# A hybrid attention and DeltaNet layer on one core: products of ones ahead of the tokens, norm weights spread by TensorE, the first head's K and V as plain products, and small products issued in groups

## The chip, the core and the metric

The kernel runs on one core of one Trainium2 chip. The metric is the device time of one execution in microseconds (us). The program lays out the inputs on the host beforehand; what is timed is one launch. In what follows PE is TensorE, DVE is VectorE, ACT is ScalarE, POOL is GpSimd and SP is SyncE, whose queue issues nearly all DMAs.

## The reference, cut to what matters

The layer takes 512 tokens of width 1024 and puts 16 learned meta tokens ahead of them, so L = 528. Everything is float32.

```python
hn = rms_norm(h, norm_w)                      # h: (1, 528, 1024)
proj = hn @ w_in                              # 1024 x 10256
aq, ak, av, az, dq, dk, dv, dz, db, da, ga, gd = split(proj)
...
s = q_blk . k * dh**-0.5                      # 8 heads, two maps of 64 each
p = softmax(where(causal, s, -inf))
o_a = (p[0] - lam * p[1]) @ v                 # differential attention
y_a = (rms_norm(o_a) * (1 - lam_init) * silu(az)) @ w_branch_attn
...
qkv = silu(causal_conv(concat(dq, dk, dv)))   # 4 taps, then l2-normalised q, k
v_new = u_c - w_c @ state                     # gated delta rule, chunk after chunk
o_c = qd_c @ state + a_c @ v_new
state = state * cd_c + kd_c.T @ v_new
y_d = (rms_norm(o_d) * silu(dz)) @ w_branch_delta
merged = sigmoid(ga) * y_a + sigmoid(gd) * y_d
out = rms_norm(h + merged @ w_out, final_norm_w)[:, 16:]
```

## The kernel before, in words

**Precision.** A float32 product is made of three fast passes. Each operand is split into a rounded high part and the rest: the tokens into `hnH` and `hnL`, each 512 KB block of weights (`raw`, 1024 inputs by 128 outputs) into `wh` (a copy by ACT) and `wl` (a subtraction by DVE). `PASSES` are high times high, high times low and low times high. A plain product of one block (`product`, and `first_products` for the first two blocks) walks over 8 slices of the inputs, three passes each, over the segments `FULL` of 272 and 256 tokens: 24 matmuls of 272 columns and 24 of 256.

**Pairs.** Two blocks whose number stands in `PAIRS` (line 60) go together through `pair_of_blocks`: seven half products in place of eight, in the manner of Strassen, of 264 columns each, from sums of tokens (`sumH`, `sumL`, made once by `token_sums`) and sums of weights, which DVE makes for each pair (`split_pair`). A pair takes 7 x 4 x 3 = 84 matmuls of 264 columns. The K and V blocks of the attention (`ak`, `av`) of every head are such a pair.

**Start.** `loads` (line 498) issues from SP's queue the first 128 tokens (`xt`), the norm weights spread over all partitions (`nwb`, 512 KB written to SBUF), the meta tokens (`mt`), the second 128 tokens, and then weights and tokens in turns. `normalise(n)` (line 526) takes the tokens as they land: ACT squares and sums a row, DVE scales the sum (`ss`), POOL takes the power (`rs`), DVE writes `dg`, the identity times `rs`; the inner task `weigh` multiplies `xt` by `nwb` on DVE; PE multiplies `xt` slice by slice with `dg`, which transposes and normalises in one; ACT copies the result to `hnH` and DVE subtracts to get `hnL`. n = 0 is the meta tokens, 1 to 4 are the 128-token pieces. `first_products` (line 1812) then starts the first two blocks (`dk` of heads 0 and 1) slice by slice as tokens come.

**Order of the work.** Every instruction is recorded through one helper, `Engine.emit`, so all rows of the profile have one line, L231 in this kernel. The program is written as tasks (Python generators) that say which engine, buffer or event they want next. A planner (`class Plan`) gives each instruction an estimated duration, takes over and over the task whose next step could begin earliest (`run`; equal times go by rank), and so writes the order in which instructions stand in each engine's queue. On the chip each engine runs its queue in that order and waits where an operand is late. `COLD` (line 80) is the planned time before which the planner counts PE's work double. Dense work (the products of tokens and weights) is one task of low priority, `dense`; attention (`attention`) and the delta rule (`delta_pair`, four pairs of heads) put small products of 128 columns or fewer, mostly between three dense passes, wherever their operands are planned to be there.

**Small chains.** In `delta_pair` a chunk's step runs from `S,kT` on PE over `vin` on DVE to `vin,TM` on PE, over `u` on ACT to `u,ktd` on PE, which gives the next state. In `attention`, `scores` writes `ak,aq` into the two-bank PSUM tile `psc`, ACT exponentiates to `e`, `combine` transposes and multiplies by `vs`, and the part of the meta tokens is `vm` times `pmT`.

**PSUM.** Six single banks go round under three kinds (`pd`, `pat`, `pdl`); `psc` is apart. `first_products` uses two banks for block 0 and `psc` for both segments of block 1.

## Time and profile before

| | |
|---|---|
| median of 3 runs | 757.45 us (757.4 to 757.57) |
| the profiled execution | 757.24 us |
| its span, first to last instruction | 755.5 us |
| PE busy | 735.5 us, 97% |
| DVE busy | 626.2 us, 83% |
| ACT busy | 498.6 us, 66% |
| first PE instruction | at 7.45 us |
| last PE instruction | begins at 748.89 us |

The span leaves 1.74 us of the profiled execution's time outside it. In the rows of the trace a first number is the start in us from the span's start, then the duration, engine, line, operation, output and inputs by the program's names, the tile (for a matmul the stationary part), and the output's shape; `xN` says that N records of one kind stand together, and a bracket tells how long the engine stood idle before and for what. A float32 matmul (`dg,xt`, `S,kT`) leaves two records, one per pass; a pass of the split products leaves one. Matmuls overlap, so what a pass costs is the distance from one start to the next, not its duration.

### The profile page before, as it was taken

The numbers are of one execution on the slowest core, as the hardware profiler recorded it, in microseconds if no ns is written. First come the engines' busy times: TensorE is split into PE (matmuls) and PEld (weight loads), VectorE is DVE, ScalarE is ACT, GpSimd is POOL, SyncE is SP. The second block draws the span as 40 slices with busy tenths as digits, with TensorE's granted clock in tenths as the row PEclk, the third lists the DMA queues.
The fourth block names the chain that finished last, engine by engine and source line by source line (L and its number), as shares of the span: only waits on it lengthen the run. The fifth ranks groups of instructions, "written<-read, shape, count | busy, mean of one in ns | idle before, by whom it ended". The sixth has DMA issues, their size and how long they took to land.

```text
span 755.5 us, 14370 instructions
## 1 busy us (share of the span) xinstructions
PE 735.5 (97%) x5311; PEld 668.6 (88%) x5311; DVE 626.2 (83%) x1431; ACT 498.6 (66%) x1322; POOL 74.7 (10%) x86
## 2 busy tenths in 40 slices
PE   5999999999999999999999999999999999999996
PEld 5998888899899899989989989988988998899875
DVE  6999999998889789879989888997479869797453
ACT  6369565879965678976767797767675445545132
POOL 3205000202000301100030210010000000000001
PEclk9999999999999999999999999999999999999998
DMA  8141321225314112521331152152141443132602
GB/s 306 57 133 33 114 80 64 64 71 158 97 42 140 34 53 85 169 78 52 110 79 59 36 180 85 56 202 65 49 147 57 141 130 121 56 118 90 239 4 109
DMA packets 45431, 74.88 MB, mean 99 GB/s; under 512 B 20728, under 2 KB 25636, under 8 KB 45360
## 3 DMA queue, kind: packets, MB, share of 16 engines
q1 hardware_dynamic: 45360, 73.95, 30.8%
q8 instruction: 42, 0.69, 0.4%
q14 instruction: 29, 0.24, 0.1%
HBM read 67.58 MB, written 6.36 MB: 98 GB/s over the span
## 4 chain that ended last, share of the span: by engine, by line
PE 83%; ACT 8%; DVE 4%; issue 2%; DMA 1%; POOL 0%; SPq 0%; POOLq 0%; ACTq 0%
PE bank L231 80%; PE psc L231 3%; ACT wh L231 2%; DVE wl L231 1%; ACT TM L231 1%; ACT ak L231 1%; DMA xt<-in_x_dram 1%; ACT vr L231 0%; DMA raw<-in_wblk_dram 0%; ACT bank L231 0%; ACT MT L231 0%; ACT e L231 0%; ACT aq L231 0%; ACT sqk L231 0%; DVE hnL L231 0%
## 5 line engine op out<-in xcount | busy, mean ns | idle before, releaser
L231 PE MATMUL bank<-hnH,wh 128*128 128x512 f32 (+4 forms) x664 | 233.4, 355 | 0.7 <-ACT hnH L231 0.7
L231 PE MATMUL bank<-hnH,wl 128*128 128x512 f32 (+4 forms) x664 | 221.6, 337 | 0.0
L231 PE MATMUL bank<-hnL,wh 128*128 128x512 f32 (+4 forms) x664 | 221.5, 337 | 0.0
L231 DVE TENSOR_TENSOR wl<-raw,wh 128x1024 fp32r<-128x1024 f32 (+1 forms) x120 | 134.9, 1126 | 24.6 <-ACT wh L231 24.1
L231 ACT CAST wh<-raw 128x1024 fp32r<-128x1024 f32 (+1 forms) x120 | 116.3, 971 | 43.4 <-PE bank L231 36.0
L231 PEld LDWEIGHTS bank<-hnH,wl 128*128 128x128 f32 x664 | 124.1, 188 | 13.9
L231 PEld LDWEIGHTS bank<-hnH,wh 128*128 128x128 f32 x664 | 124.5, 189 | 13.4 <-ACT hnH L231 0.9
L231 PEld LDWEIGHTS bank<-hnL,wh 128*128 128x128 f32 x664 | 124.4, 189 | 10.0
L231 PE MATMUL bank<-sumH,wh 128*128 128x264 f32 x224 | 68.5, 306 | 0.0
L231 PE MATMUL bank<-sumH,wl 128*128 128x264 f32 x224 | 63.6, 284 | 0.0
L231 PE MATMUL bank<-sumL,wh 128*128 128x264 f32 x224 | 63.5, 284 | 0.0
L231 DVE SCALAR_TENSOR_TENSOR y<-xp,pc,y 128x528 f32<-128x528 f32 (+1 forms) x72 | 54.0, 753 | 1.1 <-ACT y L231 1.0
L231 ACT ACTIVATE e<-psc,ast 128x144 f32<-128x144 f32 (+3 forms) x64 | 34.7, 543 | 21.5 <-DVE ast L231 18.3
L231 PEld LDWEIGHTS bank<-sumH,wh 128*128 128x128 f32 x224 | 42.3, 189 | 1.1 <-issue 0.6
L231 PEld LDWEIGHTS bank<-sumL,wh 128*128 128x128 f32 x224 | 42.4, 189 | 0.0
L231 PEld LDWEIGHTS bank<-sumH,wl 128*128 128x128 f32 x224 | 42.1, 188 | 0.0
L231 PE MATMUL bank<-btH,wh 128*128 128x256 f32 x128 | 36.1, 282 | 0.5 <-ACT sn L231 0.5
L231 PE MATMUL bank<-btH,wl 128*128 128x256 f32 x128 | 35.8, 280 | 0.0
L231 PE MATMUL bank<-btL,wh 128*128 128x256 f32 x128 | 35.8, 280 | 0.0
L231 ACT CAST wh<-st 128x1024 fp32r<-128x1024 f32 x22 | 23.1, 1048 | 13.0 <-PE bank L231 12.8
L231 PE MATMUL psc<-ak,aq 128*128 128x264 f32 (+3 forms) x160 | 29.7, 305 | 0.8 <-DVE aq L231 0.4
L231 DVE TENSOR_TENSOR wl<-st,wh 128x1024 fp32r<-128x1024 f32 x22 | 26.8, 1218 | 3.4 <-ACT wh L231 1.9
(373 smaller groups left out, 1699.5 us busy)
## 6 DMA issues: line engine op xcount, KB each, us to landing
raw<-in_wblk_dram SPq DMA_DIRECT2D x96, 512.0 KB, 3.5
raw<-in_wout_dram SPq DMA_DIRECT2D x8, 512.0 KB, 5.1
xt<-in_x_dram SPq DMA_DIRECT2D x4, 512.0 KB, 4.8
TM<-gcd SPq DMA_DIRECT2D x8, 256.0 KB, 5.2
xr<-in_x_dram SPq DMA_DIRECT2D x8, 256.0 KB, 6.3
out_dram<-xr SPq DMA_DIRECT2D x8, 256.0 KB, 2.5
room<-scrm SPq DMA_DIRECT2D x12, 128.0 KB, 3.3
oad<-room SPq DMA_DIRECT2D x6, 256.0 KB
```

What stands on the lines that cost most here:

```text
L231: return real(*args, **kw)
```

## The change

It has five parts.

1. The spread load of the norm weights is gone. One row of 4 KB (`nrow`) is loaded from ACT's queue as the kernel's first DMA. A new task, `norm_weights`, has PE multiply ones by ones eight times into `psc`, then spread the row over 128 partitions with two matmuls of a column of ones (K = 1) into the two banks of `psc`. `weigh` reads `psc`: the first 128 tokens in two halves, the others in one. `psc` is given back when all four are weighed.
2. `COLD` is 5200 in place of 10500, and the planner tells dense tasks from the others. While dense work can go on, small products wait until the dense run has lasted 300 ns (rank 0) or 900 ns (other ranks); after a small product, dense work is put off by 80 ns in the comparison; a change from small to dense is charged 85 ns.
3. The pair of `ak` and `av` of head 0 is out of `PAIRS`: the two blocks are plain products, and `after_a` copies them out.
4. `first_products` takes a single bank for block 1's first segment and waits for halves of `hnH`. `ss`, `rs` and `dg` have five buffers in place of three.
5. `combine` multiplies `vm` by `pmT` last and not first; `delta_pair` waits for the token sums' `t3` before it fetches `msub`.

```diff
-PAIRS = [n for n, (name, i) in enumerate(ORDER) if name == "ak" or name in ("dk", "dv") and i > 1 and i % 2 == 0]
+PAIRS = [n for n, (name, i) in enumerate(ORDER) if name == "ak" and i > 0 or name in ("dk", "dv") and i > 1 and i % 2 == 0]
...
-COLD = 10500
+COLD = 5200
+DENSE = ("dense", "rest_of_gates", "attention")
+SWITCH, RUNS, STAY = 85, (300, 900), 80
...
     def resume(self, task, engine, begin):
+        if engine == PE and self.dense(task) != self.run_kind:
+            self.run_kind, self.run_since = not self.run_kind, begin
+            begin += SWITCH * self.run_kind
...
+            steady = self.run_kind and any(
+                t.want == PE and self.dense(t) and t.time + (t.src != PE) * (self.HOP[t.src] + 80) <= self.free[PE]
+                for t in self.tasks)
...
-                key = max(t, self.free[eng]), task.rank
+                if eng == PE and steady and not self.dense(task):
+                    t = max(t, self.run_since + RUNS[task.rank > 0])
+                begin = max(t, self.free[eng])
+                key = begin + STAY * (eng == PE and not self.run_kind and self.dense(task)), task.rank
...
-    nwb = mk(sp, [P, D], F32, "nwb")
+    nrow = mk(sp, [1, D], F32, "nrow")
+    nc.scalar.dma_start(out=nrow, in_=prow[:, 1296:2320])
+    plan.events["nrow"] = 3200.0, SP
...
-                S.dma_start(out=nwb, in_=prow[:, 1296:2320].broadcast_to([P, D]))
-                done("nwb")
-                yield SP
...
-            yield "nwb"
-            yield DVE
-            V.tensor_tensor(out=xt[n], in0=xt[n], in1=mt[:, P:2 * P] if n == 0 else nwb, op=ALU.mult)
+            for c, w in ((0, 1), (1, 1)) if n == 1 else ((0, 2),):
+                for hf in range(c, c + w):
+                    yield f"norm weights {hf}"
+                yield DVE
+                t = xt[n][:, 512 * c:512 * (c + w)]
+                V.tensor_tensor(out=t, in0=t, in1=late["nw"][:, c:c + w].rearrange("p a t -> p (a t)"), op=ALU.mult)
             done(f"xw{n}")
+            if tick("weighed", NC):
+                give("psc")
...
+    def norm_weights():
+        yield ("psc",)
+        yield PE
+        nw = late["nw"] = bank("psc")
+        for _ in range(8):
+            T.matmul(nw[:, 0, 0:P], ones, ones, start=True, stop=True)
+        yield "nrow"
+        for hf in range(2):
+            yield PE
+            T.matmul(nw[:, hf], ones[0:1], nrow[:, 512 * hf:512 * hf + 512], start=True, stop=True)
+            done(f"norm weights {hf}")
...
+        yield "t3"
         msub = room[1].rearrange("p a t -> p (a t)")[:, 0:D].rearrange("p (j i) -> p j i", i=32)
...
-            T.matmul(po[:, 0:P], pmT, late["vm"], start=True, stop=False)
             for n in range(i + 1):
-                T.matmul(po[:, 0:P], pT[:, n, :], vs[:, n, :], start=False, stop=n == i)
+                T.matmul(po[:, 0:P], pT[:, n, :], vs[:, n, :], start=n == 0, stop=False)
+            T.matmul(po[:, 0:P], pmT, late["vm"], start=False, stop=True)
...
+    AFTER = dict(dk=after_dk, dv=after_dv, dq=after_dq, aq=after_aq, ak=lambda h, banks: after_a(h, banks, whole_ak),
+                 av=lambda h, banks: after_a(h, banks, whole_av))
```

The order that the planner writes changes over the whole length of PE's queue; the lines of the changed kernel read L252. Three places matter below. The first is the head of PE's queue. Before it reads as follows (`ss,samb` sums the meta tokens' squares, `dg,xt` transposes tokens, `wh` and `wl` belong to the first two blocks):

```order
L231 MATMUL bank_3_80<-ss_182,samb_96 128x1
...
L231 MATMUL bank_3_80<-dg_188,xt_123 128x128 x4
L231 MATMUL bank_4_81<-dg_188,xt_123 128x128 x4
L231 MATMUL bank_1_78<-hnH,wh_19_116 128x272 x8
L231 MATMUL bank_1_78<-hnH,wl_20_117 128x272 x3
L231 MATMUL bank_5_82<-dg_193,xt_124 128x128 x4
L231 MATMUL bank_6_83<-dg_193,xt_124 128x128 x4
L231 MATMUL bank_1_78<-hnH,wl_20_117 128x272 x5
L231 MATMUL bank_1_78<-hnL,wh_19_116 128x272 x8
L231 MATMUL psc_175<-hnH,wh_21_118 128x272 x3
L231 MATMUL bank_3_80<-dg_198,xt_125 128x128 x4
```

The same place in the changed kernel:

```order
L252 MATMUL psc_176<-ones 128x128 x8
L252 MATMUL psc_176<-nrow_84,ones 128x512 x2
...
L252 MATMUL bank_3_80<-dg_196,xt_124 128x128 x4
L252 MATMUL bank_4_81<-dg_196,xt_124 128x128 x4
L252 MATMUL bank_1_78<-hnH,wh_19_117 128x272 x7
L252 MATMUL bank_5_82<-dg_201,xt_125 128x128 x4
L252 MATMUL bank_6_83<-dg_201,xt_125 128x128 x4
L252 MATMUL bank_1_78<-hnH,wh_19_117 128x272
L252 MATMUL bank_1_78<-hnH,wl_20_118 128x272 x8
L252 MATMUL bank_1_78<-hnL,wh_19_117 128x272 x8
L252 MATMUL bank_3_80<-hnH,wh_21_119 128x272 x8
L252 MATMUL bank_3_80<-hnH,wl_22_120 128x272 x7
L252 MATMUL bank_4_81<-dg_206,xt_126 128x128 x4
```

Ten products stand ahead of everything, and between the second and the last piece of tokens 39 products of 272 columns stand where 27 stood.

The second place is the head of DVE's queue, from the weighing of the first tokens to the last `dg`. Before, the third piece's `dg_193` stands behind a `wl` and four `hnL`:

```order
L231 TENSOR_TENSOR hnL<-bank_4_81,hnH 128x4x128
L231 TENSOR_SCALAR ss_191<-ss_191 128x1
L231 TENSOR_TENSOR xt_124<-xt_124,nwb_84 128x1024
L231 TENSOR_TENSOR hnL<-bank_5_82,hnH 128x4x128
L231 TENSOR_TENSOR hnL<-bank_6_83,hnH 128x8x16
L231 TENSOR_TENSOR hnL<-bank_3_80,hnH 128x4x128
L231 TENSOR_TENSOR wl_22_119<-raw_15_112,wh_21_118 128x1024
L231 TENSOR_TENSOR hnL<-bank_4_81,hnH 128x4x128
L231 TENSOR_SCALAR dg_193<-ident,rs_192 128x128
```

In the changed kernel:

```order
L252 TENSOR_TENSOR hnL<-bank_4_81,hnH 128x4x128
L252 TENSOR_SCALAR ss_199<-ss_199 128x1
L252 TENSOR_TENSOR hnL<-bank_5_82,hnH 128x4x128
L252 TENSOR_TENSOR hnL<-bank_6_83,hnH 128x8x16
L252 TENSOR_SCALAR dg_201<-ident,rs_200 128x128
L252 TENSOR_TENSOR xt_125<-xt_125,psc_176 128x1024
L252 TENSOR_TENSOR hnL<-bank_3_80,hnH 128x4x128
L252 TENSOR_TENSOR hnL<-bank_4_81,hnH 128x4x128
L252 TENSOR_TENSOR wl_22_120<-raw_15_113,wh_21_119 128x1024
```

The third piece's `dg_201` has moved ahead of two `hnL`, the second `wl` and its own weighing; what stands up to the fourth piece's `dg` is the same work in both.

The third place is the first step of the delta rule on PE (`S` is the state, `kT` the keys, one of each head). Before, with dense passes (`hnH,wh` and the like) between:

```order
L231 MATMUL bank_6_83<-S_1769,kT_549 128x128
L231 MATMUL bank_1_78<-hnH,wh_19_116 128x264
L231 MATMUL bank_1_78<-hnL,wh_19_116 128x264
L231 MATMUL bank_1_78<-hnH,wl_20_117 128x264
L231 MATMUL bank_5_82<-S_1775,kT_604 128x128
L231 MATMUL bank_1_78<-hnH,wh_19_116 128x264
L231 MATMUL bank_1_78<-hnL,wh_19_116 128x264
L231 MATMUL bank_1_78<-hnH,wl_20_117 128x264
...
L231 MATMUL bank_6_83<-vin_1912,TM_680 128x128
L231 MATMUL bank_5_82<-vin_1915,TM_680 128x128
```

In the changed kernel:

```order
L252 MATMUL bank_6_83<-S_1750,kT_556 128x128
L252 MATMUL bank_5_82<-sumH_36_136,wh_23_121 128x264
L252 MATMUL bank_5_82<-sumL_40_140,wh_23_121 128x264
L252 MATMUL bank_5_82<-sumH_36_136,wl_24_122 128x264
L252 MATMUL bank_3_80<-S_1760,kT_597 128x128
L252 MATMUL bank_6_83<-vin_1881,TM_738 128x128
...
L252 MATMUL bank_3_80<-vin_1892,TM_738 128x128
```

The first head's `vin` stands directly behind the second head's `S,kT`, with three dense passes between it and its own `S,kT` where there were nine. Over the whole queue, runs of small products that stand between dense passes number 188 where there were 217.

More of the change, by code (lines that the diff above doesn't have):

```diff
@@ L142, in transfer, with dense @@
         self.arrival = self.dma + 900
+    def dense(self, task):
+        return task.gen.__name__ in DENSE and not task.other
     def resume(self, task, engine, begin):
+        if engine == PE and self.dense(task) != self.run_kind:
+            self.run_kind, self.run_since = not self.run_kind, begin
+            begin += SWITCH * self.run_kind
         self.task, self.engine, self.end, self.arrival = task, engine, begin, 0.0
@@ L982, in whole_av, with after_a @@
         done(f"av{h}")
+    def after_a(h, banks, then):
+        yield "ap"
+        yield ("vT",)
+        which = plan.task.slot
+        for j in range(2):
+            yield banks.event(j)
+            yield ACT
+            pd, t0, w = banks[j]
+            A.copy(out=late["vT"][which][:, t0:t0 + w], in_=pd)
+            give("pd", pd)
+        yield from then(h, which)
     kt_, s_, sd_, vs_, qe_ = 0, 1, 2, 3, 4
@@ L1812, in first_products @@
     def first_products():
-        yield ("psc",)
-        sc = bank("psc")
-        dst = [[], (sc[:, 0, :], sc[:, 1, :])]
+        dst = [[], []]
         for _ in range(2):
@@ L1822, in first_products @@
             for n in range(2):
+                if n == 1 and hb == 0:
+                    yield ("pd",)
+                    dst[1].append(bank("pd"))
+                if n == 1 and hb == 1:
+                    yield ("psc",)
+                    dst[1].append(bank("psc")[:, 0])
                 pd = dst[n][hb][:, :nn]
```

29 lines of the change are left out of this document (20 added, 9 removed).

## The prediction

> **What bounds the kernel now.** I read the head of the page first, then the busy time by stretches, then PE's waits.
>
> ```profile
> span 755.5 us, 14370 instructions
> PE 735.5 (97%) x5311; PEld 668.6 (88%) x5311; DVE 626.2 (83%) x1431; ACT 498.6 (66%) x1322; POOL 74.7 (10%) x86
> PE 83%; ACT 8%; DVE 4%; issue 2%; DMA 1%; POOL 0%; SPq 0%; POOLq 0%; ACTq 0%
> ```
>
> PE is busy for 97% of the span and carries 83% of the chain that ended last. The time is PE's passes plus the holes between them, so each part of the change has to be priced as passes added, passes removed and holes.
>
> ```profile
> 0.00:20.00 20.00, 11.40 (x66) 10.88 (x67) 13.06 (x27) 12.22 (x22) 7.67 (x18) 1.00 0.84 307
> 60.00:80.00 20.00, 19.70 (x122) 17.09 (x120) 18.94 (x35) 16.63 (x41) 9.14 (x3) 1.00 0.11 31
> 527.00:743.00 216.00, 215.54 (x1324) 190.83 (x1323) 156.35 (x271) 106.69 (x207) 4.84 (x5) 1.00 0.32 105
> ```
>
> The columns behind the length are PE, PEld, DVE, ACT and POOL. There are three kinds of stretch. In the first 20 us PE works for 11.40 us. Around the first attention (60 to 80 us) DVE is busy for 18.94 of 20 us. In the last third nothing but PE matters (215.54 of 216), and there only passes count.
>
> ```profile
> PE bank L231 <- ACT st L231: 7.5, 1, 7.5
> PE bank L231 <- DVE qT L231: 1.0, 2, 0.7
> PE psc L231 <- DVE aq L231: 0.4, 1, 0.4
> PE bank L231 <- DVE tdmt L231: 0.4, 1, 0.4
> PE psc L231 <- ACT e L231: 0.3, 1, 0.3
> PE bank L231 <- DVE vin L231: 0.4, 1, 0.4
> ```
>
> Of PE's waits after the start (total, times, longest), those of at least 0.3 us that hang on the first attention and on DVE's late queue there are qT, aq, tdmt and e: 2.1 us together. The named waits are few and short, so there is not much to win after 37 us.
>
> **The start.** What was in the queues until the fourth piece of tokens:
>
> ```profile
> 7.45 0.59 PE L231 MATMUL bank<-ss,samb 128*128 128x1 f32 x2 [7.45 <-ACT st L231]
> 8.13 3.78 PE L231 MATMUL bank<-dg,xt 128*128 128x128 f32 x16
> 11.70 0.63 PE L231 MATMUL bank<-dg,mt 128*128 128x128 f32 x2
> 12.13 2.95 PE L231 MATMUL bank<-dg,xt 128*128 128x128 f32 x16
> 14.84 0.75 PE L231 MATMUL bank<-hnH,wh 128*128 128x272 f32 x4
> ...
> 21.80 1.16 PE L231 MATMUL bank<-dg,xt 128*128 128x128 f32 x8
> 22.72 1.11 PE L231 MATMUL bank<-hnH,wbs 128*32 128x272 f32 x7
> ```
>
> Sixteen passes from 8.13 to 11.70 cost 223 ns each; eight from 21.80 to 22.72 cost 115. The sixteen from 12.13 to 14.84 took 2.71 us, which is 8 at 223 and 8 at 115, so PE came to speed at about 13.9 us, 6.5 us after its first pass. (The granted clock reads 1.00 in the stretch; the distances are the better witness.) The two rates are the price of an early PE.
>
> ```profile
> 0.92 0.17 DVE L231 MEMSET ones<- 128x128 f32 x1
> ...
> 6.65 1.23 DVE L231 TENSOR_TENSOR xt<-xt,nwb 128x1024 f32<-128x1024 f32 x1 [0.97 <-DMA nwb<-in_prow_dram]
> ...
> 9.54 1.22 DVE L231 TENSOR_TENSOR xt<-xt,nwb 128x1024 f32<-128x1024 f32 x1
> 11.19 0.29 DVE L231 TENSOR_SCALAR dg<-ident,rs 128x128 f32<-128x128 f32 x1 [0.44 <-POOL rs L231]
> ...
> 13.19 1.22 DVE L231 TENSOR_TENSOR xt<-xt,nwb 128x1024 f32<-128x1024 f32 x1
> ...
> 21.18 0.57 DVE L231 TENSOR_SCALAR dg<-ident,rs 128x128 f32<-128x128 f32 x1
> ```
>
> ```profile
> 9.70 1.46 POOL L231 TENSOR_TENSOR rs<-ss,mhalf 128x1 f32<-128x1 f32 x1 [0.73 <-DVE ss L231]
> 13.42 1.39 POOL L231 TENSOR_TENSOR rs<-ss,mhalf 128x1 f32<-128x1 f32 x1 [2.27 <-DVE ss L231]
> ```
>
> ```profile
> nwb<-in_prow_dram SPq DMA_DIRECT2D x1, 512.0 KB, 5.3
> scrm<-mtm SPq DMA_DIRECT2D x4, 4.0 KB, 2.5
> ```
>
> When does the first weighing begin after the change? The sixteen passes of ones can start when `ones` is written, at about 1.2 us, and run slow: 16 x 0.223 = 3.6, to 4.8 us. The row `nrow`, 4 KB, is issued at about 1 us; the nearest rows land in 2.5 us (4 KB) and 5.3 us (512 KB), so at 3.5 to 6.3 us; I take the small one, which the ones hide. Then come two float32 products of 512 columns, four passes. If a column costs what it costs a split pass at speed (0.126 us for 272, below), a pass takes 0.24 and the four 0.95 us; if it costs what `dg,xt` costs slow, 4 x 0.223 = 0.89 us each and 3.6 us. I take 2.2, between them, because PE comes to speed at about 1.2 + 6.5 = 7.7 us by the row and a K of 1 has no row at all: weighing from 4.8 + 2.2 + 0.2 for the signal = 7.2 us, with ends at 5.9 (4.8 + 0.95 and the signal) and 10.1 (6.3 + 3.6 and the signal). Before it was 6.65. So by my value the spread by PE is half a microsecond later than the transfer that it replaces.
>
> The Trainium skill, "TensorE: Matmul & The Clock Gate", Part 1, says that the clock is released by about 3.4 us of sustained activity, with the switch around 4 us. By it PE would be at speed at about 5.2 us, and the time would be that of the second rival below. The trace differs: its first pass was at 7.45 and the speed came at 13.9, but 16 passes with gaps ahead of them are not quite sustained work.
>
> From there DVE sets the pace. From the first to the second weighing it took 9.54 - 6.65 = 2.89 us, with waits for the meta tokens; after the change it is two halves, a `dg`, `mt` and two short `ss`, about 1.9 us. From the second weighing to its `dg` it took 1.65 us, since POOL's power (1.46 and 1.39 us in the rows) ended about 0.5 us after DVE's weighing of 1.2 us did, both times: the two do not run side by side. In the new order the powers of the meta tokens and of the second piece both fall behind that weighing, so I add 0.5 for one more of them: 2.15 us. The second `dg` is then at 7.2 + 1.9 + 2.15 = 11.25 against 11.19, and from it to the fourth `dg` stands the same work, 21.18 - 11.19 = 9.99 us. DVE gains nothing (+0.05), and each microsecond of the weighing moves it by one. What is gained is PE's: 12 products of 272 columns more stand ahead of the fourth `dg,xt` (39 for 27), in time that PE spent waiting. At 0.126 that is 1.5 us. **Start: -1.45**, with ends -2.75 (weighing at 5.9) and +1.45 (at 10.1).
>
> **Head 0 without a pair.**
>
> ```profile
> 36.45 0.29 PE L231 MATMUL bank<-hnH,wh 128*128 128x272 f32 x1
> ...
> 39.47 0.28 PE L231 MATMUL bank<-hnH,wh 128*128 128x256 f32 x1
> ```
>
> ```profile
> 82.68 0.28 PE L231 MATMUL bank<-hnH,wh 128*128 128x264 f32 x1
> ...
> 85.11 0.28 PE L231 MATMUL bank<-sumH,wl 128*128 128x264 f32 x1
> ```
>
> 24 passes of 272 columns take 39.47 - 36.45 = 3.02 us, 0.126 each; 256 columns by the same rate 0.118. From 82.68 to 85.11 lie 20 passes of 264 columns, 0.1215 each. Two plain blocks are 48 x 0.126 + 48 x 0.118 = 11.7 us against 84 x 0.1215 = 10.2. **+1.45**, certain, since PE has no hole there to put them in.
>
> ```profile
> L231 DVE TENSOR_TENSOR wl<-st,wh 128x1024 fp32r<-128x1024 f32 x22 | 26.8, 1218 | 3.4 <-ACT wh L231 1.9
> ```
>
> In return DVE loses a `wl` of summed weights (1.22 us by this group's mean) and four sums of weights half that size (by half the time, 0.6 each), together about 3.6 us, ahead of the stretch where it is busy for 18.94 of 20.
>
> That is what should make DVE arrive in time for qT, aq, tdmt and, behind them, e: of their 2.1 us I take 1.7 as gone, since the order around them is written anew and a few tenths come back. **-1.7**, with ends -2.1 and, if the new order brings its own waits, +1.0. The other waits (vin and smaller) I leave as they are.
>
> **Gathering.** What a change between dense and small costs by itself:
>
> ```profile
> 43.62 0.29 PE L231 MATMUL bank<-hnH,wl 128*128 128x272 f32 x1
> 43.75 0.27 PE L231 MATMUL bank<-ident,gc 128*32 128x128 f32 x1
> ...
> 43.99 0.29 PE L231 MATMUL bank<-hnL,wh 128*128 128x272 f32 x1
> ```
>
> From 43.62 to 43.99 stand two dense passes (0.252) and one small pass (0.115 at speed): 0.367 of 0.37 us. The change costs about nothing; 10 ns is my value for it, from the rounding of these rows. The planner's number is 85 ns. With 217 groups before and 188 after, 29 x 0.01 = **-0.3**; by the planner's number -2.5; that is the lower end, and 0 the upper.
>
> The other edits I put at nothing: `vm` last waits for the same copy by ACT that the first product now waits for; the halves of `hnH` and the extra bank are in the start; `t3` is made about when the tokens are; from 743 us on nothing is changed. Half a megabyte less to move at the start can bring tokens earlier, but in my chain they wait for the weighing anyway.
>
> **Sum.** -1.45 + 1.45 - 1.7 - 0.3 = -2.0 us: 757.24 - 2.0 = 755.2 for a profiled execution; the median of before lay 0.21 above its own, so 755.4.
>
> **Rivals.**
>
> *The change of kind is dear.* If 85 ns per group is right, gathering gives 2.5 and not 0.3: -4.2, 753.0, a median of 753.2 us. For it: the pass ahead of a small one overlaps with it in the record, so a busy PE can hide a hole. Against: the rows at 43.62.
>
> *PE comes to speed sooner.* If the rate changes when the ones end, each pass of 512 costs 4 x 0.115 = 0.46 us and the four 1.84, the weighing begins at 4.8 + 1.84 + 0.2 = 6.8 and DVE gains 0.4: -2.4, 754.8, a median of 755.0 us. The page named above speaks for it. For it: the ones are back to back, which the first passes of before were not quite. Against: 6.5 us in the row.
>
> *The spread comes late, and the ones buy nothing.* The row lands at 6.3 us, as the large one did, and the weighing begins at 8.5: the start gives 1.45 - 1.3 = 0.15, and DVE's relief, with its chain later by 1.3, gives 1.0 in place of 1.7. -0.15 + 1.45 - 0.3 - 1.0 = 0: 757.24, a median of 757.4 us. For it: the DMA engines are busy for 0.84 of the first stretch (its last column but one), and a small row can stand behind large ones there.
>
> *Slower: the gathered steps of the delta rule wait.* Where `vin,TM` follows its `S,kT` after fewer passes than the way over DVE takes, PE stands.
>
> ```profile
> 151.44 0.38 PE L231 MATMUL bank<-S,kT 128*128 128x128 f32 x2
> ...
> 152.98 0.61 PE L231 MATMUL bank<-vin,TM 128*128 128x128 f32 x4
> ```
>
> In before the way from `S,kT` to `vin,TM` had 152.98 - 151.44 = 1.54 us, nine dense passes and two small products. In the new order three dense passes and two small products stand there, about 0.8 us. If 1.1 us are needed, each of the 16 rounds (four pairs of heads, four chunks) that is placed so loses 0.3: +4.8 for all, and -2.0 + 4.8 = +2.8 gives 760.0, a median of 760.2 us. The sign turns at 2.0 / 0.3, about seven rounds, and at twelve it is slower beyond doubt. For it: vin is waited for already (0.4). Against: one wait in 32 steps, so the way is mostly short enough, and the first step in the new order is among its tightest.
>
> **How the numbers follow.** About 0.2% (1.5 us) is what a measurement of this kernel can tell from no change, so faster ends at 755.9 and slower begins at 759.0. The forecast has 0.35 (0.25 of it faster, 0.10 same), the dear change 0.18 (faster), the early speed 0.15 (0.12 faster, 0.03 same), the late spread 0.18 (0.03, 0.13, 0.02 slower), the waiting steps 0.14 (0.02 same, 0.12 slower): 0.58, 0.28, 0.14. The range goes down to the start's and the gathering's good ends together with the full relief, -2.75 + 1.45 - 2.5 - 2.1 = -5.9, 751.5, and up to 759.0, into the last rival, with less than 2 in 10 left out.
>
> **What would show it.** Right: the first `xt` product on DVE at 7.2 us; the fourth `dg` near 21.2; PE's waits for qT and aq gone from the list of waits; the first dense pass after a small one still 0.12 us after it. Wrong: a weighing at 8.5 us or later; the distance from a dense pass over a small one to the next clearly below that of before with fewer groups; waits of PE for vin or u of several tenths in many rounds. The sum fails if the span changes by more than 3 us while the start and these waits stand as forecast.

## The result, and the profile after

The changed kernel is slower. Its executions took 761.62, 761.84 and 763.47 us against a median of 757.42 us for the kernel before on the same chip: a ratio of 1.0064, 95% interval 1.0045 to 1.0084. (A fourth execution, at a mean granted clock of 0.653, took 1031.12 us; it, and one execution each of start_same_order (905.1 us) and no_gathering_faster_pe (4122.56 us) below, are left out of medians and ratios.) The forecast was 755.4 us in a range of 751.5 to 759.0, so it was wrong in sign, and the range too low.

The profiled execution took 761.84 us. The head of its page, and the same three stretches as before:

```profile
span 760.1 us, 14415 instructions
PE 744.7 (98%) x5343; PEld 674.6 (89%) x5343; DVE 615.9 (81%) x1422; ACT 498.9 (66%) x1321; POOL 72.2 (9%) x86
```

```profile
0.00:20.00 20.00, 18.07 (x106) 16.29 (x107) 13.94 (x29) 13.08 (x23) 6.95 (x21) 0.91 0.78 284
60.00:80.00 20.00, 20.00 (x126) 17.70 (x125) 19.93 (x33) 17.75 (x43) 5.61 (x4) 1.00 0.26 81
527.00:743.00 216.00, 215.54 (x1316) 190.74 (x1315) 156.57 (x269) 106.70 (x207) 3.87 (x4) 1.00 0.32 105
```

In the columns as before, PE works for 18.07 of the first 20 us, but 5.87 of these are the new ones and spread, so its other work there grew only from 11.40 to 12.20 us. From 60 to 80 us it now has no hole (19.70 before). The last third is as it was. The start of PE's queue and of DVE's:

```profile
1.14 3.78 PE L252 MATMUL psc<-ones 128*128 128x128 f32 x16 [1.14 <-DVE ones L252]
4.85 2.16 PE L252 MATMUL psc<-nrow,ones 1*128 1x512 f32 x4
6.94 0.38 PE L252 MATMUL bank<-ss,samb 128*128 128x1 f32 x2
7.99 3.19 PE L252 MATMUL bank<-dg,xt 128*128 128x128 f32 x16 [0.66 <-DVE dg L252]
10.97 0.63 PE L252 MATMUL bank<-dg,mt 128*128 128x128 f32 x2
...
33.72 0.29 PE L252 MATMUL bank<-hnH,wh 128*128 128x272 f32 x1
```

```profile
7.05 0.69 DVE L252 TENSOR_TENSOR xt<-xt,psc 128x512 f32<-128x512 f32 x1 [1.12 <-PE psc L252]
...
8.78 1.21 DVE L252 TENSOR_TENSOR xt<-xt,psc 128x1024 f32<-128x1024 f32 x1
9.91 0.47 DVE L252 TENSOR_SCALAR dg<-ident,rs 128x128 f32<-128x128 f32 x2
...
20.07 0.45 DVE L252 TENSOR_SCALAR dg<-ident,rs 128x128 f32<-128x128 f32 x1
```

The row at 33.72 is the landmark for the start: it is the first pass of the third block, behind the tokens, the first two blocks and the gates' products in both orders. Before it stood at 36.45 (quoted with the pair above), so the start gained 2.73 us. The landmark for the middle is the first pass of the first branch's product, `btH,wh`, behind all of attention and the delta rule. Its group (count, shortest, median and longest in ns, first and last start), first of before, then of after:

```profile
L231 PE MATMUL bank<-btH,wh x128: 276/280/385, 582.7 to 702.5; 128*128 128x256 f32 x128
```

```profile
L252 PE MATMUL bank<-btH,wh x128: 276/283/385, 586.9 to 707.2; 128*128 128x256 f32 x128
```

From landmark to landmark it is 582.66 - 36.45 = 546.2 us before and 586.86 - 33.72 = 553.1 after: **+6.9 us in the middle**, of which 1.45 are the passes of the unpaired head. What is behind the second landmark takes 0.4 us more. -2.7 + 6.9 + 0.4 = +4.6 is the difference of the spans.

A third landmark tells where in the middle. At one dense pass PE has done the same work in both kernels, but for the 20 passes of ones and spread and the 12 of the unpaired head; first before, then after:

```profile
123.27 0.48 PE L231 MATMUL bank<-hnH,wh 128*128 128x512 f32 x1
```

```profile
121.06 0.48 PE L252 MATMUL bank<-hnH,wh 128*128 128x512 f32 x1
```

So at 121 us the changed kernel is still 2.2 us ahead. -2.7 from the start and +1.45 of passes leave about -0.9 for the first attention, where -1.7 was forecast. All of the loss, 2.2 + 4.6 = 6.8 us, lies behind that point. It is in holes and in slow passes, and PE's waits tell a part of the holes:

```profile
PE bank L252 <- DVE tdmt L252: 1.4, 1, 1.4
PE bank L252 <- DVE kT L252: 1.0, 1, 1.0
PE psc L252 <- ACT e L252: 0.8, 2, 0.6
PE bank L252 <- DVE xp L252: 0.7, 1, 0.7
PE bank L252 <- ACT pmT L252: 0.7, 2, 0.5
PE bank L252 <- DVE vT L252: 0.5, 1, 0.5
```

The waits for qT are gone, as forecast, and in their place stand others, for work of the same engines at other places: tdmt 1.4 for 0.4 (at 131 us), and kT, xp, vT and pmT, which were not in the list. Two of them have a sequel:

```profile
428.94 0.28 PE L252 MATMUL bank<-sumH,wl 128*128 128x264 f32 x1
430.20 0.66 PE L252 MATMUL bank<-ident,kT 128*128 128x128 f32 x4 [0.99 <-DVE kT L252]
431.59 0.39 PE L252 MATMUL bank<-hnH,wh 128*128 128x264 f32 x1 [0.73 <-DVE xp L252]
...
431.95 0.42 PE L252 MATMUL bank<-hnH,wl 128*128 128x264 f32 x1
432.17 0.42 PE L252 MATMUL bank<-hnH,wh 128*128 128x264 f32 x1
...
435.25 0.33 PE L252 MATMUL bank<-hnH,wl 128*128 128x264 f32 x1
435.41 0.29 PE L252 MATMUL bank<-hnH,wh 128*128 128x264 f32 x1
```

After PE stood for 0.99 and 0.73 us within 2.7 us, the passes from 431.95 to 435.25 are 0.22 us apart and not 0.12: fifteen passes at half rate, 1.5 us more, on top of the waits.

### The profile page after: what moved, and what is told of

Its sections match the earlier page's. It is cut to its first block, busy times and chain, and to the rows that moved or that the text cites. A ratio compares the mean times of both kernels' runs of the same rounds, so it can differ in the third digit from the quotient of the medians.

```text
span 760.1 us, 14415 instructions
## 1 busy us (share of the span) xinstructions
PE 744.7 (98%) x5343; PEld 674.6 (89%) x5343; DVE 615.9 (81%) x1422; ACT 498.9 (66%) x1321; POOL 72.2 (9%) x86
## 5 line engine op out<-in xcount | busy, mean ns | idle before, releaser
L252 PE MATMUL bank<-hnH,wh 128*128 128x512 f32 (+4 forms) x692 | 240.0, 351 | 1.3 <-DVE xp L252 0.7
L252 PE MATMUL bank<-hnL,wh 128*128 128x512 f32 (+4 forms) x692 | 229.4, 336 | 0.0
L252 PE MATMUL bank<-hnH,wl 128*128 128x512 f32 (+4 forms) x692 | 229.1, 336 | 0.0
L252 DVE TENSOR_TENSOR wl<-raw,wh 128x1024 fp32r<-128x1024 f32 (+1 forms) x119 | 133.8, 1127 | 24.9 <-ACT wh L252 21.8
L252 ACT CAST wh<-raw 128x1024 fp32r<-128x1024 f32 (+1 forms) x119 | 115.4, 972 | 55.2 <-PE bank L252 45.0
L252 PEld LDWEIGHTS bank<-hnH,wh 128*128 128x128 f32 x692 | 130.2, 190 | 15.2 <-DVE xp L252 1.0
L252 PEld LDWEIGHTS bank<-hnH,wl 128*128 128x128 f32 x692 | 129.7, 189 | 14.0
L252 PEld LDWEIGHTS bank<-hnL,wh 128*128 128x128 f32 x692 | 130.0, 190 | 10.2
L252 PE MATMUL bank<-sumH,wh 128*128 128x264 f32 x208 | 62.9, 302 | 0.1
L252 PE MATMUL bank<-sumH,wl 128*128 128x264 f32 x208 | 59.0, 284 | 0.0
L252 PE MATMUL bank<-sumL,wh 128*128 128x264 f32 x208 | 59.0, 284 | 0.0
L252 DVE SCALAR_TENSOR_TENSOR y<-xp,pc,y 128x528 f32<-128x528 f32 (+1 forms) x72 | 54.4, 759 | 0.0
L252 ACT ACTIVATE e<-psc,ast 128x144 f32<-128x144 f32 (+3 forms) x64 | 34.5, 542 | 10.3 <-DVE ast L252 9.0
L252 PEld LDWEIGHTS bank<-sumH,wh 128*128 128x128 f32 x208 | 39.5, 190 | 0.6 <-ACT xp L252 0.3
L252 PEld LDWEIGHTS bank<-sumL,wh 128*128 128x128 f32 x208 | 39.3, 189 | 0.0
L252 PEld LDWEIGHTS bank<-sumH,wl 128*128 128x128 f32 x208 | 39.1, 188 | 0.0
L252 PE MATMUL bank<-btH,wh 128*128 128x256 f32 x128 | 36.3, 284 | 0.5 <-ACT sn L252 0.5
L252 PE MATMUL bank<-btH,wl 128*128 128x256 f32 x128 | 36.0, 281 | 0.0
L252 PE MATMUL bank<-btL,wh 128*128 128x256 f32 x128 | 36.0, 281 | 0.0
L252 PE MATMUL psc<-ak,aq 128*128 128x264 f32 (+3 forms) x160 | 29.9, 306 | 1.3 <-ACT e L252 0.8
L252 ACT CAST wh<-st 128x1024 fp32r<-128x1024 f32 x21 | 22.0, 1047 | 12.3 <-PE bank L252 10.4
L252 DVE TENSOR_TENSOR tmps<-room,ts 99x84 f32<-99x84 f32 (+23 forms) x124 | 27.4, 221 | 2.8 <-DMA room<-scrm 1.7
```

What stands on the lines that cost most here:

```text
L252: return real(*args, **kw)
```

## The experiments

Five theories were set against each other (A, B and C in the first set, D and E later). A: gathering itself costs. B: the time hangs on the order that the planner happens to write, and any new order of this program is a draw. C: the charge of 85 ns makes PE too slow in the plan as a whole, so that DVE's work stands too late and PE waits for it. D: the charge does harm only where it stands. E, a sharper D: the charge gives false cover to each gap between small products. In the two kernels that put these orders on the kernel before (gathering_alone and before_slower_pe) nothing waits for `t3`, so the fetch of `msub` and the token sums share a tile and the sums' values differ; the instructions are the same. The times are medians.

**First set: the parts of gathering.** The charge, hold and delay are `SWITCH`, `RUNS` and `STAY`.

```diff
 no_gathering (the changed kernel):
-SWITCH, RUNS, STAY = 85, (300, 900), 80
+SWITCH, RUNS, STAY = 0, (0, 0), 0
 gathering_alone (the kernel before):
+SWITCH, RUNS, STAY = 85, (300, 900), 80     # and the lines of resume and run that use them
 no_charge (the changed kernel):
+SWITCH, RUNS, STAY = 0, (300, 900), 80
 charge_alone (the changed kernel):
+SWITCH, RUNS, STAY = 85, (0, 0), 0
```

> The changed kernel with the charge, the hold and the delay for small products all at 0; everything else of the change stays. Theory A (gathering costs: small products held back find their operands no earlier, and the engines behind them run late): the lead of about 2.7 us that the changed kernel had at 122 us stays to the end, about 754.8 us. Theory B (any newly written order of this program costs some us, whichever rule wrote it): between 758 and 763 us, the lead lost as in the changed kernel. Theory C (the charge of 85 ns alone puts the plan out of step with the chip): 754.8 here too, but see the run without the charge.

Measured: 760.26 us (757.43 to 763.40), ratio 1.0038 (1.0014 to 1.0062). Theories A and C foresaw 754.8, B 758 to 763; without any gathering most of the loss against the forecast is still there.

> The kernel before with nothing but the gathering: the charge of 85, the hold of 300 and 900, the delay of 80 ns. Theory A: slower than before by the 6.9 us that the changed kernel lost between 122 and 557 us, less the 1.5 us of a stretch at half clock, so 762 to 764 us. Theory B: unforeseeable, within some 3 us of 757.4 on either side. Theory C: about 761 us.

Measured: 765.56 us, 1.0104 (1.0083 to 1.0124). Above all three forecasts (A 762 to 764, B at most about 760, C about 761), and nearest to A.

> The changed kernel with the charge at 0; the hold of 300 and 900 and the delay of 80 ns stay. Theory A: still slow, 760 to 763 us. Theory C: about 755 us. Theory B: unforeseeable, 756 to 763 us.

Measured: 758.3 us, 1.0000 (0.9988 to 1.0012). Better than with the charge and not the 755 of C; B had allowed it (756 to 763), A had not.

> The changed kernel with the hold and the delay at 0; the charge of 85 ns stays. Theory A: about 755 us, as without gathering. Theory C: 760 to 763 us. Theory B: unforeseeable, 756 to 763 us.

Measured: 768.8 us, 1.0139 (1.0118 to 1.0159). The slowest of the four, and above every forecast made for it. So A falls as it stood: in these four orders the hold and the delay without the charge cost nothing that shows, the charge goes with the slow ones, and yet its absence doesn't bring the forecast back.

**Second set: the plan's clock, another draw, the pair.** One factor on PE's durations in the plan, `COLD`, and `PAIRS`; the first, second and fourth without the charge, the third without any gathering.

```diff
 plan_slower_pe, plan_faster_pe (no_charge, with 1.02 and 0.98):
-            self.plan.spend(self.name, self.time(op, args, kw) * slow)
+            self.plan.spend(self.name, self.time(op, args, kw) * slow * (1.02 if self.name == PE else 1))
 reroll (no_gathering):
-COLD = 5200
+COLD = 6000
 pair_kept (no_charge):
-... if name == "ak" and i > 0 or name in ("dk", "dv") ...
+... if name == "ak" or name in ("dk", "dv") ...
```

> The changed kernel without the charge, and every duration of PE in the plan times 1.02 (about 14 us more of PE in the plan, as much as 85 ns at each of 188 changes). Theory C (a plan in which PE is slower than on the chip lets DVE's work stand too late, and PE waits for DVE): slower than the 758.3 us without the charge by 3 to 8 us, with PE's waits for kT, xp, vT back. Rival D (the charge does harm only where it stands, at the small products): within 1.5 us of 758.3.

Measured: 760.81 us, 1.0032 (1.0018 to 1.0046): 2.5 more than at 1, between C and its rival D.

> The changed kernel without the charge, and every duration of PE in the plan times 0.98. Theory C: as fast as 758.3 us or faster by up to 2 us, since DVE's work is put earlier; Theory B (any new order moves the time by some us either way): anything from 755 to 762 us.

Measured: 764.17 us, 1.0086 (1.0071 to 1.0101). C's forecast was the other way, 758.3 or faster, and B's range ended at 762. A plan with a faster PE is no better by that alone.

> The changed kernel without any gathering, and with COLD at 6000 in place of 5200: the same rules, a slightly other clock at the start of the plan, and so another order from the first attention on. Theory B: differs from the 760.26 us without gathering by 2 us or more. Rival: within 1 us of it, and the order matters little where the rules are the same.

Measured: 758.94 us, 1.0014 (1.0003 to 1.0025): 1.3 from no_gathering, undecided by itself.

> The changed kernel without the charge, and with head 0's K and V as a pair, as before. By the sum of the prediction the pair saves 1.45 us of passes and costs DVE 3.6 us of work ahead of the first attention, for which PE waited 1.7 us: 758.3 + 0.25, within 1.5 us of 758.3. If DVE's relief does not matter: 756.9.

Measured: 763.78 us, 1.0079 (1.0062 to 1.0097). Neither number: 5.5 slower than with the head unpaired, though it has 1.45 us fewer passes. One edit whose own price is small by the passes moved the time by 5 us, and the whole order behind it is new. That fits B, and it means that this run does not price the pair.

**Third set: is it the order?** One kernel that adds only a start and keeps before's order; two that keep the rules of before and shift its plan; and the changed kernel with a shifted plan.

```diff
 start_same_order (the kernel before):
+    nrow = nwb[0:1]                                    # its 4 KB load first on ACT's queue
+    nw = mk(ps, [P, 2, 512], F32, "psc", SLOTS["psc"])  # the next two loops outside the plan
+    for _ in range(8):
+        nc.tensor.matmul(nw[:, 0, 0:P], ones, ones, start=True, stop=True)
+    for hf in range(2):
+        nc.tensor.matmul(nw[:, hf], ones[0:1], nrow[:, 512 * hf:512 * hf + 512], start=True, stop=True)
...
-                S.dma_start(out=nwb, in_=prow[:, 1296:2320].broadcast_to([P, D]))
+                plan.spend(SP, 60)
+                plan.transfer(4 * P * D)
...
+                for hf in range(2):                     # behind the first weighing, which reads nw
+                    nc.scalar.copy(out=nwb[:, 512 * hf:512 * hf + 512], in_=nw[:, hf])
 before_slower_pe, before_faster_pe (the kernel before), change_faster_pe (the changed kernel):
+            self.plan.spend(self.name, self.time(op, args, kw) * slow * (1.02 if self.name == PE else 1))   # 0.98
```

> The kernel before with the ones and the spread by PE ahead of the tokens, written outside the plan, so that every engine's queue is that of before but for these: eight ones and two spreads at PE's head, the row's load and two copies of the spread weights at ACT's head, no 512 KB spread on SP. The first tokens are weighed from PSUM, the others from the copy. If the start's gain is real and lasts where the order stays (theory B: what the change loses, it loses by its new order): 2.0 to 2.8 us faster than before, about 755.0. If a faster start is given back later by waits for DVE or transfers whatever the order: within 0.7 us of before.

Measured: 759.58 us, 1.0033 (1.0020 to 1.0045), slower and not faster. The start itself was worse: in the profiled execution (761.35 us) the spread's passes ran slow to the end, and the two copies stood ahead of the meta tokens' square on ACT, for which PE waited until 11.34 us. So it says nothing on whether a gain at the start would last, and something better on the order. Its first pass of the third block stood at 39.98 us, 3.5 behind before. From there on the rows are those of before, shifted; of before, and of this kernel:

```profile
73.67 0.38 PE L231 MATMUL bank<-qT,kT 128*128 128x128 f32 x1 [0.30 <-DVE qT L231]
```

```profile
80.87 0.38 PE L231 MATMUL bank<-qT,kT 128*128 128x128 f32 x1 [0.66 <-DVE qT L231]
```

```profile
77.23 0.49 PE L231 MATMUL bank<-qT,kT 128*128 128x128 f32 x2 [0.28 <-DVE qT L231]
```

```profile
84.43 0.38 PE L231 MATMUL bank<-qT,kT 128*128 128x128 f32 x1 [0.66 <-DVE qT L231]
```

```profile
L231 PE MATMUL bank<-btH,wh x128: 276/280/385, 586.6 to 706.6; 128*128 128x256 f32 x128
```

The same waits, to 0.02 us, 3.56 us later; the branch begins 3.9 later. With the order kept, 546.6 us lie between the landmarks for 546.2. A start 3.5 us later made a span 4.1 us longer, so a delay at the start is carried to the end, and **the holes belong to the order**. No run has a gain at the start with the order kept.

> The kernel before with every duration of PE in its plan times 1.02: its own rules, another order, no part of the change. Theory B: 759 to 766 us, as the other new orders came out, since the one on record is a good draw. If the rules of before make good orders whatever the draw, and only the change's rules make poor ones: 756 to 759 us.

Measured: 766.08 us, 1.0118 (1.0102 to 1.0133).

> The kernel before with every duration of PE in its plan times 0.98. As for 1.02: theory B 759 to 766 us, the rival 756 to 759 us.

Measured: 765.74 us, 1.0109 (1.0096 to 1.0122). Both as theory B had it: the rules of before, with no part of the change, write orders that are over 8 us slower when its plan's PE is shifted by 2% either way. Of these three draws by one set of rules, the order on record before is the best.

> The changed kernel, charge and hold as they are, with every duration of PE in the plan times 0.98, which takes about as much out of the plan as the charge puts in. If the charge does its harm as too slow a PE in the plan: near the 758.3 us without the charge. Theory B: another draw, 758 to 768 us, mean about 762.

Measured: 754.49 us (753.07 to 755.60), 0.9958 (0.9945 to 0.9971): faster than before and 7 to 8 us faster than the changed kernel, by one factor in the planner, and below every forecast (758.3; B's 758 to 768). Its longest waits behind the start, and its landmark:

```profile
PE bank L252 <- ACT vm L252: 0.8, 2, 0.6
PE bank L252 <- ACT sn L252: 0.5, 1, 0.5
PE psc L252 <- ACT e L252: 0.4, 1, 0.4
PE bank L252 <- DVE TM L252: 0.2, 1, 0.2
```

```profile
L252 PE MATMUL bank<-btH,wh x128: 276/280/392, 581.4 to 700.9; 128*128 128x256 f32 x128
```

No wait for tdmt, kT or xp is left. This is the version that beats both kernels; it is the best of four draws by the change's rules, not a rule found.

**Fourth set: rule or draw.** More draws by the change's rules and without gathering, on the same base, by the same factor on PE's planned durations.

```diff
 change_slower_pe, change_099_pe (the changed kernel; 1.02 and 0.99); no_gathering_faster_pe, no_gathering_slower_pe, no_gathering_104_pe (no_gathering; 0.98, 1.02 and 1.04):
-            self.plan.spend(self.name, self.time(op, args, kw) * slow)
+            self.plan.spend(self.name, self.time(op, args, kw) * slow * (1.02 if self.name == PE else 1))
```

> The changed kernel as it is, with PE's planned durations times 1.02. If the rule is poor: 761 to 768 us, as the changed kernel and the charge alone. If the draw decides: anywhere from 754 to 768 us.

Measured (1.02, all rules of the change): 774.43 us, 1.0227 (1.0207 to 1.0247), the slowest of all and above both forecasts.

> The changed kernel as it is, with PE's planned durations times 0.99. If the rule is poor unless the plan's PE is made faster: between 754.5 (at 0.98) and 762.6 (at 1), about 758. If the draw decides: anywhere from 754 to 768 us.

Measured (0.99): 766.53 us, 1.0112 (1.0068 to 1.0156), so the way from 0.98 to 1 is not even: 754.5, 766.5, 761.8. The draw had it, the poor rule's 758 did not.

> The changed kernel without any gathering, PE's planned durations times 0.98. If gathering is what costs: within 2 us of the 759 to 760 us of the two draws without it. If the draw decides: anywhere from 754 to 768 us.

Measured (0.98, no gathering): 758.15 us, 0.9991 (0.9964 to 1.0018), which both forecasts had.

> The changed kernel without any gathering, PE's planned durations times 1.02. If gathering is what costs: within 2 us of 759 to 760 us. If the draw decides: anywhere from 754 to 768 us.

Measured (1.02, no gathering): 756.0 us, 0.9981 (0.9972 to 0.9990), which only the draw had. The four draws without gathering (at most 2% on the plan) lie between 756.0 and 760.3, closer together than those with it.

**Last: an evenly slow plan, and the ones alone.**

> The changed kernel without any gathering, PE's planned durations times 1.04: as much PE time in the plan as the changed kernel has at 1.02 with its charge, which took 774.4 us, but spread evenly. Theory C (too slow a PE in the plan as a whole): 766 us or more. Theory E (the charge gives false cover of 85 ns to each gap between small products, where an even 4% of a gap of three passes is 15 ns): 755 to 761 us, like the other draws without gathering.

```diff
 ones_same_order (the kernel before, outside the plan):
+    nw = mk(ps, [P, 2, 512], F32, "psc", SLOTS["psc"])
+    for _ in range(8):
+        nc.tensor.matmul(nw[:, 0, 0:P], ones, ones, start=True, stop=True)
```

> The kernel before with nothing but eight products of ones at PE's head, outside the plan; every queue is otherwise that of before. By the prediction's chain DVE sets the pace from the first weighing on and a PE that is faster there only waits longer: within 0.5 us of before. If the early passes make PE fast by 7.5 us and the transposes set the pace: up to 1.5 us faster.

Measured: no_gathering_104_pe 767.17 us, 1.0126 (1.0108 to 1.0143), as C had it and E had not, though a range of draws as wide as the fourth set's (754 to 774) holds it too; ones_same_order 757.3 us, 0.9999 (0.9990 to 1.0009): the ones by themselves move nothing. The waits of the evenly slow plan, and then those of the changed kernel at 1.02:

```profile
PE bank L252 <- DVE kT L252: 3.3, 2, 1.8
PE psc L252 <- ACT e L252: 1.8, 3, 1.0
PE bank L252 <- DVE vT L252: 1.8, 2, 1.0
```

```profile
PE bank L252 <- DVE kT L252: 3.1, 3, 1.9
PE bank L252 <- ACT ao L252: 2.3, 3, 1.3
PE bank L252 <- DVE tdmt L252: 2.2, 2, 1.4
PE bank L252 <- DVE xp L252: 1.4, 3, 0.7
```

The same engines' late results stand here as in the changed kernel, kT first, at three times its size. That fits C at its strongest: where PE is about 4% too slow in the plan (evenly, or by 2% and the charge), it comes to the results of DVE and ACT before they are there. With two such kernels it is argued and not shown.

The profiled executions of all kernels, by the two landmarks (start of the third block's first pass; from there to the first `btH,wh`; for those on the change's base with the head unpaired, 1.45 us of the second are passes):

| kernel | third block at | to the branch | median us |
|---|---|---|---|
| before | 36.5 | 546.2 | 757.4 |
| ones_same_order | 36.5 | 546.2 | 757.3 |
| start_same_order | 40.0 | 546.6 | 759.6 |
| before_slower_pe, before_faster_pe | 36.6, 36.3 | 554.9, 559.2 | 766.1, 765.7 |
| gathering_alone | 36.8 | 554.3 | 765.6 |
| the change | 33.7 | 553.1 | 761.8 |
| change_faster_pe, change_099_pe, change_slower_pe | 37.1, 34.5, 33.7 | 544.4, 556.4, 569.0 | 754.5, 766.5, 774.4 |
| charge_alone | 36.1 | 555.7 | 768.8 |
| no_charge, plan_slower_pe, plan_faster_pe | 33.3, 35.5, 34.7 | 548.6, 550.8, 558.7 | 758.3, 760.8, 764.2 |
| pair_kept | 35.6 | 554.0 | 763.8 |
| no_gathering, reroll | 34.0, 35.6 | 551.4, 551.9 | 760.3, 758.9 |
| no_gathering_faster_pe, _slower_pe, _104_pe | 37.1, 35.4, 35.0 | 551.3, 546.3, 557.4 | 758.2, 756.0, 767.2 |

The second landmark is not the same point of work everywhere: in before_faster_pe, plan_faster_pe, no_gathering_faster_pe and reroll PE has 27, 27, 21 and 9 passes fewer behind it, and 168.1 to 171.1 us are left in the span where the others have 172.3 to 174.3. Their middles read 1.7 to 4.7 us too long by that, so the medians are the safer column there. Among kernels with the same point the middle spreads over 25 us, the start over 4 (without start_same_order). The number of groups of small products does not rank the kernels: before has 217, the change 188.

## Why the prediction was wrong, step by step

**The start: right in sign, short in size.** The weighing began at 7.05 us (forecast 7.2), the landmark came 2.7 us earlier (forecast 1.45, lower end 2.75). The term that was mis-sized is POOL's: I added 0.5 us because two powers would wait behind the second weighing. They did not wait; the second row here stands beside the fourth piece's weighing of 16.61 to 17.82 us:

```profile
8.88 1.07 POOL L252 TENSOR_TENSOR rs<-ss,mhalf 128x1 f32<-128x1 f32 x2 [2.32 <-DVE ss L252]
16.77 0.55 POOL L252 TENSOR_TENSOR rs<-ss,mhalf 128x1 f32<-128x1 f32 x1 [3.96 <-DVE ss L252]
```

Two powers took 1.07 us together, beside DVE's weighing of 8.78 to 9.99, where one took 1.46 before; the second `dg` began at about 10.1 (two from 9.91 on) and not at 11.25, and the fourth at 20.07 and not at 21.2. The difference is where the weights lie: the weighing of before reads two operands from SBUF, the new one has one in PSUM. start_same_order, whose second weighing reads a copy of the weights in SBUF, has a power of 1.46 us beside it again. The Trainium skill, "SBUF — State Buffer", section "SBUF: two separate sides", says that a DVE operation with two SBUF inputs and a GpSimd operation that reads SBUF exclude each other for the whole instruction; by that the trace agrees on both sides, 1.46 us with `nwb` in SBUF and about 0.54 each with `psc`. That the weighing began within 0.2 us of the forecast is in part luck. My 2.2 us for the spread's four passes was a middle between slow and fast; they took 2.09 us here (4.85 to 6.94), and of the 14 profiled executions with this start seven were like it, with a weighing at 6.6 to 7.2 us, and seven took 3.71, with a weighing at 8.7, as PE came to speed sooner or later. The landmark then came as late as 37.1 us. My end of +1.45 covered that.

**Ones alone carry nothing:** eight of them ahead of before's order moved nothing (757.3 us). That kernel has no spread, so it doesn't test the rival of an early speed, which works through the spread's passes: these took 2.09 us where that rival had 1.84 and I had 2.2, and PE did come to speed within them here. The gain stands beside the changed work behind the ones, the 12 products ahead and the freed powers.

**The unpaired head:** +1.45 of passes (by the rounded rows 11.7 - 10.2 = 1.5) follows from the passes' number and their rate, which are the same; no run prices it alone, since pair_kept had another order.

**DVE's relief: smaller than forecast, but there.** The qT waits went, and by the landmark at 121 us about 0.9 of the 1.7 us had come. Part of the rest was never there to win, since I read the list of waits without their places: in before the two of qT stand at 73.67 and 80.87 us and that of e at 106.5, but that of tdmt at 136.7, at the delta rule, and that of aq at 456.4, in a later attention. Only 1.3 of the 2.1 us hung on the first attention.

**The step that failed: "The other waits (vin and smaller) I leave as they are."** With it, all that a new order does behind the first attention was put at nothing, but for 0.3 us of gain from gathering; for new waits I had a few tenths in the relief and at most +1.0 at its end. An order written anew brings its own waits. The runs showed 6.8 us lost behind 121 us (waits for tdmt, kT, xp and others, and a stretch of slow passes), and 5.5 us in the whole middle beyond the pair's passes in place of -2.0 (relief and gathering). This was not one wait mis-sized. I priced a change of the planner's rules by the waits in the old trace, as if the rest of that order stood. The runs show that it doesn't: 2% on one number in the plan makes 766 of 757, or 754.5 of 761.8. The bound that was needed stood in no row of the trace; it needed the thought that before's order may be the best of many. The prediction's own last sign, a span off by more than 3 us while the start and these waits stand nearly as forecast, is what came.

**Gathering: 29 changes at 10 ns.** The price of a change held: in the changed kernel two dense passes of 256 columns and a small one between them take 0.35 us (44.24 to 44.59), as they do without a change. But what a change costs on the chip was beside the point; what a new order does was the size, with gathering (761.8) and without it (760.3). That the charge may put the plan's PE out of step with the chip was seen by no rival. Rival one took the charge for a price on the chip.

**The rival that ended slower** had its sign and nearly its time (760.2), by another mechanism, so by luck: PE's waits for vin and u, its witnesses, are not in the list after the change.

**How far the cause is settled.** Shown: with the order kept, the holes stay (546.2 and 546.6); with the same rules and a plan shifted by 2%, the time moves by 8 us; a plan whose PE is 4% slow is 767 us without any gathering. Open: how the 6.9 us of the middle divide. By the table, 1.45 are passes; beyond that the two draws without gathering at the same point of work, no_gathering and no_gathering_slower_pe, lie 3.7 above before's order and 1.4 below it, so a rule's share can't be told from a draw's.

Open too: whether the charge is poor as a rule. Six kernels with it (gathering_alone among them, on before's base) took 754.5 to 774.4 us, mean 765.3; seven without it on the change's base, with the head unpaired and at most 2% on the plan, 756.0 to 764.2, mean 759.5. The sets overlap, and between -2% and +2% no trend with the plan's speed is seen. Before's own rules gave 757.4, 765.7 and 766.1, mean 763.1, and all rules of the change 754.5, 761.8, 766.5 and 774.4, mean 764.3: as sets of rules the two are not told apart.

A rival to a pure draw was not tested: PE's longest wait for tdmt is 1.1 to 2.0 us in 11 of the 14 orders on the change's base, and at most 0.4 in the four orders on before's base. So that wait may belong to one of the change's other parts. Why one order is good was not found.

## What to carry to other kernels

Where a planner writes the order, a change of its numbers is a new draw: run several shifted plans before and after it and compare the sets, and do not price it by the waits of one old trace. If an order is good, keep it: put the new instructions outside the plan, as in start_same_order, and the rest repeats: the waits shown there to 0.02 us, the whole distance to the branch to 0.4. A forecast for such a change should carry the spread of draws in its range (here 754 to 774 us), not the sum of the old waits.

## What the runs showed of the hardware that was not expected

**Short holes can halve PE's rate.** In the changed kernel 0.99 and 0.73 us of standing were followed by 3.3 us at half rate. In another kernel (reroll) one wait was:

```profile
132.59 0.40 PE L252 MATMUL bank<-vrm,tdmt 32*32 32x128 f32 x2 [1.95 <-DVE tdmt L252]
...
133.33 0.42 PE L252 MATMUL bank<-hnH,wl 128*128 128x264 f32 x1
133.55 0.42 PE L252 MATMUL bank<-hnH,wh 128*128 128x264 f32 x1
```

The same followed waits of 1.74 us (gathering_alone) and 1.83 us (plan_slower_pe), and not the single wait of 1.41 us of the changed kernel at 131 us. These stretches lasted from 3.3 to about 4 us and cost 1.5 to 2; behind waits of 1.83 and 0.65 us within 3.3 us in no_gathering_104_pe it lasted 5.9. In before the longest wait behind the start is 0.7 us, and it has no such stretch. But a wait of this length does not always do it: behind 1.73 us (before_slower_pe), 1.85 (charge_alone), 1.91 (change_slower_pe) and 1.97 (no_gathering_faster_pe) the passes were 0.12 us apart at once or after the first one or two. And no_gathering has twelve passes at half rate from 270.04 to 272.91 us behind 4 us of small products without a wait (the last one, of 1.28 us, had ended at 264.97). So a wait of 1.7 to 2 us cost its own length or nearly twice that, and no run shows what decides. The Trainium skill, "TensorE: Matmul & The Clock Gate", section "Why this matters for your kernels", asks for gaps of no more than about 3 us between bursts; here 1.7 us within such a time was enough in some cases.

**An early PE does not stay fast.** In the changed kernel the sixteen passes from 7.99 to 10.97 us took 186 ns each on average, between the 223 and 115 ns of a slow and a fast PE in before, though the spread's passes ahead of them had come to speed (2.09 us for four) and only 0.66 us of standing lay between.
